# Differential attention: the difference of the two softmaxes on GpSimd, the eviction of the transposed probabilities on VectorE

## Chip, core and metric

The kernel runs on one core of one Trainium2 chip. The metric is the device time of one execution in microseconds, the median of several runs. Engines are called PE (TensorE), DVE (VectorE), ACT (ScalarE), POOL (GpSimd) and SP (SyncE, which issues the transfers).

## What is computed

A two-layer backbone over 256 context and 256 latent tokens of width 1024: layer 0 has scan and retention heads and a dense feed-forward, layer 1 has differential attention and two of eight experts per token. Everything is in 32-bit floats. The change lies in the attention of layer 1 alone, which has 8 heads; each head has two maps of keys and queries (64 wide each), 256 latent queries and 512 keys:

```python
def diff_attend(q, k, v, lam):
    s = jnp.einsum('bqhmd,bkhmd->bhmqk', q, k).astype(jnp.float32)
    p = jax.nn.softmax(s, axis=-1)
    a = p[:, :, 0] - lam.astype(jnp.float32) * p[:, :, 1]
    return jnp.einsum('bhqk,bkhe->bqhe', a.astype(v.dtype), v)
```

The output of a head is then normalised by its root mean square and goes through the output projection; after that a router picks experts and the weights of all eight experts are read.

## The kernel before

Layer 1 projects keys, queries and values, runs attention over heads 0 to 3 (the first half) and normalises and transposes those heads' outputs (`attended(0)`), does a little for the router, runs heads 4 to 7 and `attended(1)`, and then multiplies with the output projection (L194 to L196 with `oh`, three matmuls for each product of split operands). Weights come as 128x1024 tiles that ACT and DVE split into a high and a low part (L183, L184).

Attention itself is a loop over heads and, inside, over the two tiles of 128 queries: sixteen steps, called steps 0 to 15 here. A step, for each of its two maps m, forms 128x512 scores on PE (L1138) in one of four PSUM banks (`mm`, two for each query tile), takes the negated row maximum on DVE (L1139) and the exponential with its row sum on ACT (L1141) into tile `s0` or `s3`. The softmaxes are not divided out: the difference is kept in units of the first map's sum, so one factor per row, -lambda times the first sum over the second, is formed on DVE (L1143 the reciprocal, L1144 the product), and L1145 computes p0 = p1 * factor + p0 in one DVE instruction. L1147 puts the norm's epsilon into the same units. Four PE transposes (L1151) turn p0 by 128-column blocks into one PSUM bank (`tr`, two banks), L1153 evicts that bank to `s1` or `s2` on ACT, four accumulating matmuls multiply by the values (L1156), and ACT takes the sum of squares and the copy of the result (L1158, L1160).

Tiles `s0`, `s3` and the statistics `ast` have two buffers each, so two steps are in flight. The order of the instructions on each engine is not written out: a scheduler plans it when the kernel is built, from the dependences, the free buffers and the order of the program, and each engine then runs its list in that order. Transfers are issued from SP's list in the same way. The experts' first weights are loaded ahead into the big tiles as these come free; among them are those of the keys (`kT1`) and of the queries and outputs.

Of the kernel before, what the change touches and what calls it, by code (L numbers as in the profile page):

```python
# [14 lines left out]
AF = mybir.ActivationFunctionType  # L15
ALU = mybir.AluOpType
# [949 lines left out]
class Layer1(Layer0):  # L966
# [159 lines left out]
    def attention(self, heads):  # L1126

        nc = self.nc
        v = nc.vector
        for h in heads:  # L1130
            for t in range(2):
                qs = slice(P * t, P * t + P)
                st = self.scr("ast", (P, 6))
                p = []
                for m in range(2):
                    r = slice(64 * m, 64 * m + 64)
                    ps = self.mm(2 * t + m)
                    nc.tensor.matmul(ps, self.qT1[r, h, qs], self.kT1[r, h, :], start=True, stop=True)  # L1138
                    v.tensor_reduce(st[:, m:m + 1], ps, axis=AX.X, op=ALU.max, negate=True)  # L1139
                    e = self.scr(f"s{3 * m}")  # L1140
                    nc.scalar.activation(e, ps, AF.Exp, bias=st[:, m:m + 1], accum_out=st[:, 2 + m:3 + m])  # L1141
                    p.append(e)
                v.reciprocal(st[:, 4:5], st[:, 3:4])  # L1143
                v.scalar_tensor_tensor(st[:, 5:6], st[:, 2:3], self.lam, st[:, 4:5], op0=ALU.mult, op1=ALU.mult)  # L1144
                v.scalar_tensor_tensor(p[0], p[1], st[:, 5:6], p[0], op0=ALU.mult, op1=ALU.add)  # L1145

                v.scalar_tensor_tensor(self.o_eps[:, h // 4, t, h % 4:h % 4 + 1], st[:, 2:3], EPS, st[:, 2:3],  # L1147
                                       op0=ALU.mult, op1=ALU.mult)
                pt = self.tr()
                for c in range(4):  # L1150
                    nc.tensor.transpose(pt[:, P * c:P * c + P], p[0][:, P * c:P * c + P], self.ident)  # L1151
                at = self.scr(f"s{1 + t}")
                nc.scalar.activation(at, pt, AF.Copy)  # L1153
                po = self.acc()
                for c in range(4):
                    nc.tensor.matmul(po[:, 0:P], at[:, P * c:P * c + P], self.v1[:, c, P * h:P * h + P],  # L1156
                                     start=c == 0, stop=c == 3)
                nc.scalar.activation(self.scr("s5", (P, D), BF16)[:, 0:P], po[:, 0:P], AF.Square,  # L1158
                                     accum_out=self.o_ss[:, h // 4, t, h % 4:h % 4 + 1])
                nc.scalar.activation(self.o[:, t, P * h:P * h + P], po[:, 0:P], AF.Copy)  # L1160
# [398 lines left out]
```

## Time and profile before

| | us |
|---|---|
| median of 3 runs (1999.22 to 1999.8) | 1999.28 |
| the profiled execution | 1992.13 |
| its span, first to last instruction | 1990.0 |
| mean granted clock of TensorE, share of full | 0.988 |
| attention in the profiled span | about 1012 to 1083 |

The span is cut into 40 slices on the page, and each digit there is the busy share of an engine in tenths. Groups of instructions are named by line, engine and operation, with the tile written and the tiles read. The timeline gives the start and the duration of an instruction (or of several alike in a row, with their count) and in brackets the idle time of its engine before it and what ended that. Granted clock 1.00 is 2.4 GHz, 0.50 is 1.2 GHz.

### The profile page before, as it was taken

The page shows a single profiled execution, that of the slowest core. Times are in us where ns is not written, and L with a number is a line of the kernel's source. Part 1 is how long each engine was busy: PE and PEld are TensorE (multiplying, and loading weights), DVE is VectorE, ACT ScalarE, POOL GpSimd, SP SyncE. Part 2 cuts the span into 40 slices and gives each one's busy share as a digit, 9 for nine tenths or more (in the row PEclk, how much of TensorE's full clock was granted, in tenths as well). Part 3 has the DMA queues.
Part 4 walks back from the last instruction along what each step waited for, and adds up shares of the span by engine and source line. Part 5 has one row for each costly group of instructions (what it writes and reads, how often), then busy time and mean ns, then how long its engine had stood idle before and what let it go on. Part 6 is the DMA issues. An engine that isn't in the chain of part 4 may idle for free.

```text
span 1990.0 us, 26467 instructions
## 1 busy us (share of the span) xinstructions
PE 1909.2 (96%) x9936; PEld 1385.0 (70%) x9936; DVE 1120.0 (56%) x2011; ACT 815.4 (41%) x1286; POOL 10.1 (1%) x12
## 2 busy tenths in 40 slices
PE   6999999999999999999999999999999999999986
PEld 4776777778788888877766755876488656876341
DVE  5568668845876565667856306971298307970000
ACT  5535355542423322235455215861287316860100
POOL 0000000000000000000000000000000000000100
PEclk9999999999999999999998799999999999999999
DMA  8332434442655455532433499999999999999997
GB/s 322 118 96 96 148 117 142 145 143 75 203 166 172 154 173 189 178 101 85 132 133 113 160 418 418 416 355 394 417 417 393 364 417 417 417 340 411 417 417 316
DMA packets 103863, 502.67 MB, mean 253 GB/s; under 512 B 13104, under 2 KB 13744, under 8 KB 69296
## 3 DMA queue, kind: packets, MB, share of 16 engines
q1 hardware_dynamic: 103728, 500.91, 66.8%
q8 instruction: 80, 1.31, 0.3%
q14 instruction: 55, 0.45, 0.1%
HBM read 495.62 MB, written 5.24 MB: 252 GB/s over the span
## 4 chain that ended last, share of the span: by engine, by line
PE 74%; DMA 16%; DVE 6%; ACT 3%; issue 1%; SPq 0%; ACTq 0%; DVEq 0%
PE mm L195 16%; PE mm L196 16%; PE mm L194 16%; PE mm L1451 7%; DMA wide<-exp_d 5%; DMA wide<-exp_gu 5%; DMA raw<-exp_d 3%; PE acc L195 2%; PE acc L196 2%; PE acc L194 2%; DVE lo L184 1%; PE acc L315 1%; PE tr L1362 1%; PE acc L1465 1%; PE tr L1478 1%
## 5 line engine op out<-in xcount | busy, mean ns | idle before, releaser
L183 ACT ACTIVATE hi<-raw 128x1024 fp32r<-128x1024 f32 x208 | 220.2, 1060 | 402.6 <-PE mm L196 197.8
L184 DVE TENSOR_TENSOR lo<-raw,hi 128x1024 fp32r<-128x1024 f32 x208 | 253.7, 1223 | 175.3 <-ACT hi L183 169.9
L184 DVE TENSOR_TENSOR lo<-wide,hi 128x1024 fp32r<-128x1024 f32 x202 | 244.9, 1224 | 22.2 <-ACT hi L183 5.9
L183 ACT ACTIVATE hi<-wide 128x1024 fp32r<-128x1024 f32 x202 | 212.7, 1061 | 52.8 <-PE mm L196 34.0
L1451 PE MATMUL mm<-wide,q 128*64 128x256 f32 x1760 | 212.6, 386 | 8.5 <-DMA wide<-exp_gu 8.4
L1451 PEld LDWEIGHTS mm<-wide,q 128*64 128x64 f32 x1760 | 125.0, 138 | 82.8 <-DMA wide<-exp_gu 14.3
L194 PE MATMUL mm<-hi,hh 128*128 128x512 f32 x416 | 168.2, 405 | 1.7 <-DVE b L856 1.3
L195 PE MATMUL mm<-lo,hh 128*128 128x512 f32 x416 | 164.4, 395 | 0.1
L196 PE MATMUL mm<-hi,hl 128*128 128x512 f32 x416 | 163.3, 395 | 0.0
L1456 DVE TENSOR_TENSOR s<-s,mm 128x256 f32<-128x256 f32 x35 | 14.8, 422 | 252.1 <-ACT s L1454 252.1
L194 PE MATMUL mm<-h2h,hi 128*128 128x512 f32 (+1 forms) x376 | 142.2, 378 | 1.3 <-ACT hi L183 1.3
L195 PE MATMUL mm<-h2l,hi 128*128 128x512 f32 (+1 forms) x376 | 141.5, 377 | 0.0
L196 PE MATMUL mm<-h2h,lo 128*128 128x512 f32 (+1 forms) x376 | 141.1, 376 | 0.0
L195 PE MATMUL mm<-lo,q 128*128 128x512 f32 x336 | 133.0, 396 | 1.3 <-DVE lo L184 1.3
L196 PE MATMUL mm<-hi,q 128*128 128x512 f32 x336 | 131.3, 391 | 0.0
L1465 PE MATMUL acc<-wide,ef 128*64 128x512 f32 x456 | 111.7, 600 | 17.0 <-DMA wide<-exp_d 16.9
L194 PE MATMUL mm<-hi,q 128*128 128x512 f32 x336 | 112.9, 392 | 0.0
L194 PEld LDWEIGHTS mm<-hi,hh 128*128 128x128 f32 x416 | 78.2, 188 | 27.6 <-issue 9.7
L1465 PEld LDWEIGHTS acc<-wide,ef 128*64 128x64 f32 x456 | 32.8, 136 | 87.8 <-issue 52.2
L195 PEld LDWEIGHTS mm<-lo,hh 128*128 128x128 f32 x416 | 78.3, 188 | 17.0 <-issue 2.0
L196 PEld LDWEIGHTS mm<-hi,hl 128*128 128x128 f32 x416 | 78.0, 188 | 16.8 <-issue 0.8
L341 DVE SCALAR_TENSOR_TENSOR s<-raw,cond,s 128x512 f32<-128x512 f32 x112 | 80.4, 749 | 1.2
(393 smaller groups left out, 3243.7 us busy)
## 6 DMA issues: line engine op xcount, KB each, us to landing
wide<-exp_gu SPq DMA_DIRECT2D x177, 1024.0 KB, 14.4
wide<-exp_d SPq DMA_DIRECT2D x91, 1024.0 KB, 15.0
raw<-exp_gu SPq DMA_DIRECT2D x92, 512.0 KB, 14.7
raw<-odd_wmod SPq DMA_DIRECT2D x48, 512.0 KB, 4.2
raw<-w_in SPq DMA_DIRECT2D x44, 512.0 KB, 3.7
raw<-ffn_gu SPq DMA_DIRECT2D x44, 512.0 KB, 4.4
raw<-exp_d SPq DMA_DIRECT2D x42, 512.0 KB, 15.1
raw<-even_wmod SPq DMA_DIRECT2D x36, 512.0 KB, 3.8
```

The source lines that it names most:

```text
L183: nc.scalar.activation(hi, raw, AF.Copy)
L184: nc.vector.tensor_tensor(lo, raw, hi.bitcast(F32), op=ALU.subtract)
L194: mm(ps, lh, rh, start=first, stop=False, skip_group_check=skip)
L195: mm(ps, lh, rl, start=False, stop=False, skip_group_check=skip)
L196: mm(ps, ll, rh, start=False, stop=last, skip_group_check=skip)
L315: nc.tensor.matmul(ps[r:r + 32, :], self.cond[:, k, :], raw[:, 512 * kk:512 * kk + 512], start=k < 4, stop=k >= 4)
L341: nc.vector.scalar_tensor_tensor(t, w, self.cond[:, k, i:i + 1], t, op0=ALU.mult, op1=ALU.add)
L1362: nc.tensor.matmul(pt[:, w * kk:w * kk + w], self.x[:, 2 + t, P * (k + kk):P * (k + kk) + P], pn[:, t, 0:w], start=t == 0, stop=t == 1)
L1451: behind = mm(ps[s, 256 * g:256 * g + 256], xg[:, k, :], raw[i][:, c:c + 256], start=k + g == 0, stop=k == KD - 1, skip_group_check=True)
L1456: v.tensor_tensor(t, sg, ps[:, 256:512], op=ALU.mult)
L1465: mm(py[s], ap[:, f, :], raw[f - u][:, 512 * j:512 * j + 512], start=f == 0, stop=f == nd - 1, skip_group_check=True)
L1478: mm(pt, pT[s, P * t:P * t + P], y[s], start=True, stop=True)
```

## The change

The fused DVE instruction L1145 is replaced by two POOL instructions, a multiply of p1 by the factor (in place) and an add into p0; the eviction L1153 goes from ACT to DVE. Tiles, buffers and everything else in the program stay as they are; the planned order is made anew with the changed engines.

```diff
                 v.reciprocal(st[:, 4:5], st[:, 3:4])
                 v.scalar_tensor_tensor(st[:, 5:6], st[:, 2:3], self.lam, st[:, 4:5], op0=ALU.mult, op1=ALU.mult)
-                v.scalar_tensor_tensor(p[0], p[1], st[:, 5:6], p[0], op0=ALU.mult, op1=ALU.add)
+                nc.gpsimd.tensor_scalar(p[1], p[1], st[:, 5:6], None, op0=ALU.mult)
+                nc.gpsimd.tensor_tensor(p[0], p[0], p[1], op=ALU.add)
...
                 at = self.scr(f"s{1 + t}")
-                nc.scalar.activation(at, pt, AF.Copy)
+                v.tensor_copy(at, pt)
```

## Rows read from the trace of the kernel before

**Rows 1.** The page's slices: busy tenths of PE, busy share of the DMA engines.

```profile
PE   6999999999999999999999999999999999999986
...
DMA  8332434442655455532433499999999999999997
```

**Rows 2.** Windows: stretch, length, busy us (instructions) of PE, PEld, DVE, ACT, POOL, clock, DMA.

```profile
1012.00:1083.00 71.00, 64.27 (x301) 39.70 (x299) 43.78 (x117) 42.72 (x135) 0.00 (x0) 0.86 0.25 97
...
1144.00:1990.00 846.00, 802.96 (x4641) 522.27 (x4640) 376.10 (x392) 344.72 (x454) 9.93 (x8) 1.00 0.98 397
```

**Rows 3.** Timeline of SP's queue, the stretch from attention to the first expert.

```profile
1015.89 67.64 SPq L1401 DMA_DIRECT2D wide<-exp_gu  x6
...
1135.39 3.45 SPq L176 DMA_DIRECT2D raw<-exp_gu  x4
```

**Rows 4.** Chain that ended last, 1012 to 1084 us: shares by line.

```profile
by line: PE mm L1138 23.5%; PE acc L1156 19.9%; ACT s L1141 10.6%; PE tr L1151 10.1%; DVE ast L1139 8.9%; DVE s L1145 3.0%; issue 2.5%; PE acc L1174 2.3%; ACT s L1158 2.2%; ACT s L1153 2.1%; DVE lo L184 1.7%; PE tr L1083 1.5%; ACT hi L183 1
```

**Rows 5.** Groups, 1012 to 1083 us: xcount | busy us, mean ns | idle before, releasers.

```profile
L1145 DVE SCALAR_TENSOR_TENSOR s<-s,ast,s 128x512 f32<-128x512 f32 x16 | 12.0, 747 | 0.2
...
L1153 ACT ACTIVATE s<-tr 128x512 f32<-128x512 f32 x16 | 9.6, 601 | 3.5 <-PE tr L1151 3.5
```

**Rows 6.** Groups of POOL over the whole span.

```profile
L1415 POOL TENSOR_TENSOR rest<-x,rest 128x512 f32<-128x512 f32 x4 | 5.1, 1277 | 1883.0 <-ACT rest L358 1883.0
```

**Rows 7.** Groups of DVE: one input, two inputs, a copy out of PSUM.

```profile
L339 DVE TENSOR_SCALAR s<-raw,cond 128x512 f32<-128x512 f32 x16 | 7.6, 480 | 0.0
...
L1077 DVE TENSOR_TENSOR b<-b,ors 128x512 f32<-128x512 f32 x2 | 1.3, 687 | 0.0
...
L790 DVE COPY b<-tr 128x512 f32<-128x512 f32 x4 | 2.8, 688 | 4.0 <-PE tr L784 4.0
```

**Rows 8.** Timeline of POOL: the second instruction reads what the first wrote.

```profile
1890.82 1.27 POOL L1415 TENSOR_TENSOR rest<-x,rest 128x512 f32<-128x512 f32 x1
1892.18 1.27 POOL L1416 TENSOR_TENSOR rest<-rest,x 128x512 f32<-128x512 f32 x1
```

**Rows 9.** Timeline: difference and first transposes of steps 0 and 15.

```profile
1017.72 0.75 DVE L1145 SCALAR_TENSOR_TENSOR s<-s,ast,s 128x512 f32<-128x512 f32 x1
...
1018.68 1.05 PE L1151 MATMUL tr<-con,s 128*128 128x128 f32 x4
...
1078.24 0.75 DVE L1145 SCALAR_TENSOR_TENSOR s<-s,ast,s 128x512 f32<-128x512 f32 x1
...
1079.71 0.60 PE L1151 MATMUL tr<-con,s 128*128 128x128 f32 x4
```

**Rows 10.** Timeline of PE: products of two steps, first and last of the projection.

```profile
1067.91 1.06 PE L1156 MATMUL acc<-v,s 128*128 128x128 f32 x8
...
1070.45 1.06 PE L1156 MATMUL acc<-v,s 128*128 128x128 f32 x8
...
1076.75 0.47 PE L194 MATMUL mm<-hi,oh 128*128 128x512 f32 x1
...
1102.89 0.40 PE L196 MATMUL mm<-hi,oh 128*128 128x512 f32 x1
```

**Rows 11.** Windows of 2 us, columns as in rows 2.

```profile
1016.00:1018.00 2.00, 1.37 (x4) 0.59 (x4) 1.97 (x8) 1.87 (x5) 0.00 (x0) 1.00 1.02 420
1018.00:1020.00 2.00, 2.00 (x8) 0.99 (x6) 1.97 (x6) 0.48 (x3) 0.00 (x0) 0.70 0.81 303
...
1024.00:1026.00 2.00, 2.00 (x5) 0.68 (x3) 0.08 (x1) 1.68 (x7) 0.00 (x0) 0.59 0.51 213
...
1050.00:1052.00 2.00, 0.94 (x2) 0.29 (x2) 1.97 (x8) 0.78 (x2) 0.00 (x0) 1.00 0.00 0
1052.00:1054.00 2.00, 0.79 (x2) 0.50 (x2) 1.93 (x6) 0.78 (x2) 0.00 (x0) 0.73 0.00 0
...
1066.00:1068.00 2.00, 2.00 (x8) 0.95 (x7) 0.21 (x2) 1.74 (x7) 0.00 (x0) 0.85 0.00 0
```

**Rows 12.** Who waited for whom, 1012 to 1083 us: us, times, longest.

```profile
PE tr L1151 <- DVE s L1145: 0.2, 1, 0.2
```

## The prediction

> **What bounds the kernel now.** Read the slices of the page first [rows 1]: PE is busy nearly throughout, and from slice 23 (1144 us) to the end the DMA engines are full. Then two stretches of the windows [rows 2]: from 1144 us on the DMA share is 0.98, so the last 846 us take what the expert weights take; attention (1012 to 1083 us) has a DMA share of 0.25. Next the issuing queue [rows 3]: SP stands 67.64 us in a group of weight loads that begins at 1015.89 us, since the room they go to holds the keys of attention, and it resumes after its next long stop at 1135.39 us, when the first expert has begun to empty buffers. So the full-DMA stretch starts a fixed time after attention has ended: a microsecond lost or won on the way through attention is one at the end, and no transfer hides it.
>
> Inside attention no engine is full: in 71 us PE shows 64.27 busy, DVE 43.78, ACT 42.72 [rows 2]. The chain of waits over it [rows 4] alternates between PE (the scores L1138 23.5%, the products L1156 19.9%, the transposes L1151 10.1%), ACT and DVE. Of the two steps that change, it holds L1145 with 3.0% and L1153 with 2.1%; the window is 72 us, so 2.2 and 1.5 us. That is little beside their 12.0 and 9.6 us of busy time [rows 5]: most of each already lies beside PE.
>
> **The change part by part.** Sixteen times (8 heads by 2 query tiles):
>
> 1. *Removed from DVE:* L1145, 747 ns [rows 5], 12.0 us in all.
> 2. *Added to POOL:* a multiply of 128x512 by a column and an add of two such tiles. The add is priced by POOL's own row, 1277 ns for that shape and type [rows 6]. The multiply has no row on POOL. It is bounded below by DVE's one-input row, 480 ns [rows 7], and above by POOL's two-input 1277 ns. The nearest row is POOL's; but the multiply reads one tensor fewer, and on DVE that step goes from 687 to 480 ns, a factor of 0.70, so I take 1.27 x 0.70 = 0.89 us. Between a POOL instruction and the one that needs its result lie 0.09 us (1890.82 + 1.27 to 1892.18) [rows 8]. Together 0.89 + 0.09 + 1.27 = 2.25 us in place of 0.75: the difference p comes **1.5 us later** (1.1 with the low price, 1.9 with the high one).
> 3. *Moved from ACT to DVE:* the eviction, 601 ns on ACT [rows 5], 688 on DVE by its copy of the same shape out of the same kind of bank [rows 7]. So DVE's load stays (747 out, 688 in) and ACT's falls by 9.6 us.
>
> The Trainium skill speaks against part 2: "GPSIMD Engine Reference", section 4.1, sends elementwise work to the Vector engine, with GpSimd about two times slower for two inputs and roughly at line rate for one. The trace agrees on two inputs, 1.27 against 0.69 us. By that rate for one input (512 elements at the 1.2 GHz of the page's section 1, and some start) the multiply would be an estimated 0.6 us, and the sum below some 1.8 us lower; no run here shows that row yet.
>
> *Who waits.* Behind p on PE stand the four transposes of the same step; behind them in PE's order the scores of the step after next and the products. How much room a step has is read from the timeline: end of L1145 to the first L1151 of the same step. The first and the last of the sixteen pairs are shown [rows 9]. In order the gaps are 0.2, 2.9, 3.7, 1.7, 0.15, 0.16, 0.9, 0.7, then for the second half 13.3, 8, 4.1, 2.4, 0.7, 1.8, 0.7, 0.7 us. The wide ones lie where TensorE runs at half clock or where attention's halves meet. 0.15 is the bare hand-over, so the room is the gap less 0.15, and 1.5 us more come short by 1.45, 1.5, 1.5, 0.7, 0.9 (steps 0, 4, 5, 6, 7) and 0.95, 0.9, 0.9 (12, 14, 15): 8.8 us if all pass on. From that:
> - Steps 14 and 15 (1.8 us): beside them PE already takes up matmuls of the output projection, which at first need only the first four heads; its first L194 stands at 1076.75 and its last L196 at 1102.89 [rows 10]. What is pulled forward into the wait isn't missing later. Cost nothing; 1.8 us if the cover fails.
> - Step 0: the scores of step 2 (PE, 1.05 us at full clock, 2.0 at half) need only the exponentials, so they can go ahead of the late transposes: 1.0 of 1.45 covered.
>
> 8.8 - 1.8 - 1.0 = 6.0 us lost. *Gained:* an eviction on ACT waits there behind exponentials, and exponentials behind it; its 1.5 us on the chain [rows 4] go. L1145's 2.2 us on the chain are there because reductions of later steps queue behind it on DVE. The eviction takes that place, and it waits for PE, so I count nothing for them (2.2 us of gain if it finds a gap). **Sum: +4.5 us**; with the low price of the multiply the same sum gives +2.0, with the high one +7.4.
>
> *Queues and buffers.* POOL has no other work from its start to 1883 us [rows 6], so its wait for the factor (L1144) holds up nothing. On DVE the eviction waits for the transposes, and the reductions (L1139) and the factors of later steps stand behind it; ACT's exponentials wait for those. The statistics tile and the second exponential's tile (two buffers each) come free by POOL's instructions instead of L1145, some 0.1 and 1.5 us later; their next writers come two steps on. Steps follow each other at 2.54 us where they are fastest (products at 1067.91 and 1070.45 [rows 10]), so that is 5 us on; and POOL's 2.16 us of work fit into a step, barely. No DMA is moved past anything.
>
> **Rivals.**
> *Half clock.* TensorE falls from 2.4 to 1.2 GHz twice in attention [rows 11]: behind a slice in which PE was busy 1.37 of 2 us, and again behind one with 0.94. By the granted clocks of the slices (0.70 down to 0.50 and back over 0.59; 0.73 down and back over 0.85) it then ran some 6.8 and 13.7 us at half. Longer waits for p between 1030 and 1047 us could bring a third such stretch, which costs half its length, 3.4 to 6.9 us, on top of 4.5: about +9.6. For it: steps 4 to 7 lose most there. Against: PE's gaps there are short today. "TensorE: Matmul & The Clock Gate", section "HAM oscillation", in the Trainium skill tells of loops in which a wait returns each round and each round starts throttled; that both falls here came behind waits agrees with it.
>
> *Hidden by another order.* The order on each engine is planned when the kernel is built; with p later, PE may be given the scores of the step after next ahead of the transposes everywhere, as I assumed for step 0. They take 1.05 us, so the tight steps (0, 4, 5, 6, 7, 12) would lose 0.45, 0.45, 0.45, 0, 0 and 0, 1.35 in all, less the 1.5 of ACT: about 0 (-1 to +2). For it: L1145 made PE wait only 0.2 us in total [rows 12]. Against: today PE takes the transposes first.
>
> *Faster.* The order falls as above and the eviction finds DVE free, so L1145's 2.2 us go as well. One of its three places on the chain is where attention's halves meet: there DVE is the limit (1050 to 1054 us: 1.97 and 1.93 busy of 2 [rows 11]) and PE waits, and with L1145 off that queue the waits ahead of the second half-clock stretch get shorter. If that halves the stretch's cost of 6.9 us, the time is 0 - 2.2 - 3.4 = -5.6 us. It decides at PE's two waits of 1050 to 1054 us: from where they are gone. Against: they hang on reductions and on the first half's norm too, which stay on DVE, and the eviction's input comes 1.5 us later than today.
>
> *The change does not do what it says:* the eviction is not cheaper on DVE (688 against 601 ns), so what is saved is ACT's time alone, and ACT, at 42.72 of 71 us, is not the limit. That is inside the first sum.
>
> **How the numbers follow.** The profiled execution took 1992.13 us (span 1990.0 and 2.1 around it); the median of the runs is 1999.28, 7.2 more. The sum is made on the former, 1992.1 + 4.5 = 1996.6, and carried over to the median as a difference: 2003.8. Some 0.2%, 4 us, is what a measurement here can tell from no change.
> Chances: the forecast (+2.0 to +7.4) 0.50, of which 0.32 above 4 us; half clock 0.18, all above; another order 0.18, all within; faster 0.14 (-2.2 to -9), of which 0.11 below -4 us. So slower 0.32 + 0.18 = 0.50, same 0.18 + 0.18 + 0.03 = 0.39, faster 0.11. The range goes from -4.3 to +9.7, 1995.0 to 2009.0: the whole forecast, the other order and the nearer part of the half-clock and the faster case, so that some 0.18 stay outside. The forecast alone is 2001.3 to 2006.7.
>
> **What would show it.** In the changed profile: POOL's multiply near 0.9 us and its add near 1.27; p to transposes at the bare hand-over in steps 4 to 7, with PE waiting for POOL (in the table of waits, a row of transposes from POOL of some 4 to 7 us); the last score matmul, and with it SP's long stop, some 4 us later; the same shift at the first expert and at the end. If the transposes wait for POOL less than 2 us, the order has hidden it. If a slice at 0.50 stands between 1030 and 1047 us, the clock rival is in. If DVE waits for the transposes (its eviction behind PE) as long as ACT did, the gain is gone. The forecast is wrong altogether if the shift at the end is not that of the last score matmul.

## The result, and the profile after

The changed kernel takes 2025.16 us (median of 4 runs, 2017.24 to 2027.02) against 1999.25 of the kernel before on the same chip: a ratio of 1.0143, 95% interval 1.0117 to 1.017. Timed again later, it gave 2015.93 against 1995.5, 1.010 (1.0063 to 1.0137). So it is 25.9 and 20.4 us slower by the medians, 20 to 29 by the ratios; the prediction was 4.5 us slower, and 2009.0 at most.

The profiled execution took 2017.24 us, with a span of 2015.5 and a mean granted clock of 0.981 (before 1992.13, 1990.0 and 0.988). Line numbers behind the change are one higher: L1145 is now the multiply and L1146 the add on POOL, L1148 the epsilon, L1152 the transposes, L1154 the eviction, L1157 the products. The page's slices, to be held against [rows 1]:

```profile
PE   7999999999999999999988999999999999999986
POOL 0000000000000000000053000000000000000100
PEclk9999999999999999999978799999999998999999
DMA  8333434442655555424322499999999999989997
```

Counted from 0, attention lies in slices 20 and 21, where POOL now shows 5 and 3 tenths. The DMA row is full from slice 23 on, as before; but a slice is longer now, so that this is at 1159 us and not at 1144. The windows (columns as in [rows 2]) give attention of the changed kernel and the rest behind it:

```profile
1011.00:1102.00 91.00, 72.72 (x297) 43.19 (x296) 46.56 (x116) 35.75 (x118) 45.08 (x32) 0.81 0.20 76
...
1163.00:2015.50 852.50, 809.88 (x4640) 524.70 (x4636) 376.06 (x392) 344.23 (x454) 9.91 (x8) 0.99 0.98 393
```

The last window is laid so that it holds as many matmuls as the last one of [rows 2], 4640 and 4641; it takes 852.5 against 846 us, and most of that difference comes back below. What grew most is attention: 20 us longer, with 45.08 us of POOL in it, and the clock down from 0.86 to 0.81. The instructions of one line, from first to last start, tell its ends: scores and products of the changed kernel, then the first matmul of the experts, and below that SP's long stop.

```profile
L1138 PE MATMUL mm<-kT,b x64: 589/693/1220, 1011.1 to 1092.5; 64*128 64x512 f32 x64
...
L1157 PE MATMUL acc<-v,s x128: 273/275/582, 1025.7 to 1101.3; 128*128 128x128 f32 x128
...
L1452 PE MATMUL mm<-wide,q x1760: 378/379/690, 1139.8 to 1967.8; 128*64 128x256 f32 x196
...
1014.52 87.88 SPq L1402 DMA_DIRECT2D wide<-exp_gu  x6
```

Before, the same three were 1012.5 to 1074.9, the last product at 1081.9, and the first expert matmul at 1121.4. So attention, from its first score to its last product, grew from 69.4 to 90.2 us, **20.8 us**; SP's stop ends at 1102.40 in place of 1083.53 [rows 3], 18.9 later (attention begins 1.4 us earlier); the first expert matmul comes 18.4 later. From there the shift stays at 18.6 to 18.7 us until some 1670 us. Most of the rest, 6 us, arises in one spot between two experts:

```profile
1672.00:1674.00 2.00, 1.40 (x2) 0.50 (x2) 1.68 (x2) 1.59 (x2) 0.00 (x0) 0.65 1.00 414
1674.00:1676.00 2.00, 2.00 (x4) 1.16 (x4) 1.29 (x2) 0.00 (x0) 0.00 (x0) 0.50 1.04 430
```

TensorE falls to half clock there until 1687 us, in this execution and not in the one of before. Nothing ties it to the change: from first to last expert matmul the kernels of this study take 821.8 to 832.7 us in one profiled execution each, in no relation to what was edited that these profiles show (822.0 before, 828.0 after, 826.1 in a second profile of the changed kernel).

**What became of the parts.** Groups of the changed kernel in attention: POOL's pair, then on DVE the reductions, the eviction and the factor.

```profile
L1145 POOL TENSOR_SCALAR s<-s,ast 128x512 f32<-128x512 f32 x16 | 25.0, 1562 | 1052.2 <-DVE o_eps L1148 1033.2 <-DVE ast L1144 6.9 <-PE mm L1138 5.7
L1146 POOL TENSOR_TENSOR s<-s,s 128x512 f32<-128x512 f32 x16 | 20.2, 1262 | 1.2
...
L1139 DVE TENSOR_REDUCE ast<-mm 128x1 f32<-128x512 f32 x32 | 21.8, 688 | 18.7 <-PE mm L1138 12.3 <-POOL s L1145 6.1
L1154 DVE COPY s<-tr 128x512 f32<-128x512 f32 x16 | 11.0, 690 | 17.0 <-PE tr L1152 17.0
L1144 DVE SCALAR_TENSOR_TENSOR ast<-ast,lam 128x1 f32<-128x1 f32 x16 | 4.3, 266 | 1.8 <-ACT s L1141 1.5
```

The add (1262 ns) and the eviction (690) are as priced; the multiply is not: 1562 ns, above the upper bound of 1277 [rows 6]. And DVE stands idle 17.0 us ahead of its evictions, where ACT stood 3.5 [rows 5]. The table of waits of the same stretch:

```profile
DVE s L1154 <- PE tr L1152: 17.0, 15, 3.8
...
PE tr L1152 <- POOL s L1146: 11.3, 9, 2.5
ACT s L1141 <- PE tr L1152: 9.8, 5, 2.4
POOL s L1145 <- DVE ast L1144: 6.9, 4, 3.1
DVE ast L1139 <- POOL s L1145: 6.1, 7, 1.7
```

The chain over attention, which in [rows 4] went from PE to ACT and DVE, now goes through POOL, and the eviction, which the sum had taken off it, stands on it with 3.0% of 94 us, 2.8 us against 1.5 before:

```profile
by line: PE mm L1138 15.7%; POOL s L1145 13.7%; POOL s L1146 12.1%; PE tr L1152 11.6%; PE acc L1157 10.2%; issue 8.2%; DVE ast L1139 6.3%; DVE s L1154 3.0%; DVE ast L1144 2.5%; PE acc L1175 1.8%; PE mm L194 1.7%; PE mm L196 1.7%; ACT s L114
```

One turn of the timeline shows how these hang together:

```profile
1048.90 1.26 POOL L1146 TENSOR_TENSOR s<-s,s 128x512 f32<-128x512 f32 x1
...
1050.22 0.65 PE L1152 MATMUL tr<-con,s 128*128 128x128 f32 x4 [2.10 <-POOL s L1146]
...
1050.91 0.69 DVE L1154 COPY s<-tr 128x512 f32<-128x512 f32 x1 [1.36 <-PE tr L1152]
1051.52 0.21 DVE L1144 SCALAR_TENSOR_TENSOR ast<-ast,lam 128x1 f32<-128x1 f32 x1
...
1051.90 1.56 POOL L1145 TENSOR_SCALAR s<-s,ast 128x512 f32<-128x512 f32 x1 [1.74 <-DVE ast L1144]
```

PE waits for POOL's add (of step 6), DVE's eviction waits for PE, the factor of the next step stands behind that eviction in DVE's list, and POOL idles 1.74 us for the factor. It is a circle over three engines, in which each waits for the one before it, and it closes from one step to the very next. The chain over attention goes from an eviction by way of the factor to POOL's multiply five times (three times in the second profile of the changed kernel, below). In DVE's list the eviction of the step before stands ahead of the factor in 8 of 15 steps (in 5 where the eviction alone was moved). In other turns the circle closes without the eviction. Here the chain goes from the add of step 5 to the multiply of step 6: the scores of step 7 stand behind the transposes on PE, and the reduction that waits for them stands ahead of step 6's factor on DVE.

```profile
1042.94 1.27 POOL s L1146
...
1044.26 0.65 PE tr L1152 x4
1044.91 1.11 PE mm L1138 x4
...
1046.07 0.69 DVE ast L1139
...
1046.87 0.23 DVE ast L1144
...
1047.26 1.57 POOL s L1145
```

**Half clock.** It has a part of its own. The first stretch, which before lasted some 6.8 us [rows 11], goes from 1021 to 1037 us, into the time for which the rival of the prediction wanted a slice at 0.50, followed by shorter ones at 1051 to 1055 and 1065 to 1079. A slice of it:

```profile
1030.00:1032.00 2.00, 2.00 (x5) 0.63 (x4) 0.52 (x1) 0.73 (x3) 1.92 (x2) 0.50 0.00 0
```

### The profile page after: what moved, and what is told of

The parts are those of the page before. It is cut to its first block, busy times and chain, and to the rows that moved or that the text cites. A ratio compares the mean times of both kernels' runs of the same rounds, so it can differ in the third digit from the quotient of the medians.

```text
span 2015.5 us, 26535 instructions
## 1 busy us (share of the span) xinstructions
PE 1925.6 (96%) x9936; PEld 1390.9 (69%) x9936; DVE 1122.1 (56%) x2011; ACT 807.8 (40%) x1270; POOL 55.2 (3%) x44
## 4 chain that ended last, share of the span: by engine, by line
PE 75%; DMA 15%; DVE 6%; ACT 2%; issue 1%; POOL 1%; SPq 0%; POOLq 0%; ACTq 0%; DVEq 0%
PE mm L195 16%; PE mm L196 16%; PE mm L194 16%; PE mm L1452 9%; DMA wide<-exp_d 6%; DMA wide<-exp_gu 4%; DMA raw<-exp_d 2%; PE acc L195 2%; PE acc L196 2%; PE acc L194 2%; DVE lo L184 1%; PE acc L315 1%; PE tr L1479 1%; PE tr L1363 1%; PE acc L1466 1%
```

## The experiments

Every row below is one profiled execution's attention (first score to last product), the time in it that TensorE ran at half clock (from the granted clock of its 2-us slices), the length less half of that, called the path here, and the ratio of the timed runs. The path is an estimate: it takes all that lies in a half-clock stretch as twice as long, waits too. A "+" says what is added to the kernel named before it.

| kernel | attention | half clock | path | ratio, 95% interval |
|---|---|---|---|---|
| before | 69.4 | 20.5 | 59.2 | 1 |
| after | 90.2 | 34.2 | 73.1 | 1.0143 (1.0117 to 1.017) |
| after, a second time | 93.6 | 44.4 | 71.4 | 1.010 (1.0063 to 1.0137) |
| before + eviction on DVE | 65.1 | 10.2 | 60.0 | 0.9983 (0.9962 to 1.0004) |
| before + difference on POOL | 79.1 | 23.9 | 67.1 | 1.0053 (1.0031 to 1.0075) |
| before + difference on POOL, two-input multiply | 75.1 | 20.5 | 64.9 | 1.0029 (1.0006 to 1.0052) |
| after, two-input multiply | 81.3 | 23.9 | 69.4 | 1.007 (1.0044 to 1.0095) |
| after + a longer pair | 95.0 | 44.4 | 72.8 | 1.0152 (1.0118 to 1.0187) |
| before + POOL beside | 73.1 | 23.9 | 61.2 | 1.0024 (1.0 to 1.0047) |
| after + more statistics tiles | 90.5 | 37.6 | 71.7 | 1.011 (1.0081 to 1.0138) |
| after + deeper tiles | 78.7 | 23.9 | 66.8 | 1.0083 (1.0055 to 1.011) |
| after + order | 84.0 | 23.9 | 72.0 | 1.01 (1.0076 to 1.0125) |
| after + both | 74.7 | 23.9 | 62.7 | 1.0056 (1.0034 to 1.0077) |
| difference on POOL + DVE reader | 80.6 | 17.0 | 72.1 | 1.0086 (1.0052 to 1.012) |
| after + scores twice | 129.9 | 51.2 | 104 | 1.0282 (1.0248 to 1.0316) |
| before + eviction on DVE, order | 68.9 | 23.9 | 57.0 | 0.9981 (0.9962 to 1.0) |
| before + eviction on DVE, deeper tiles | 61.4 | 10.2 | 56.3 | 0.9955 (0.9937 to 0.9974) |

The kernel before alone varied from 1986.7 to 2004.4 us over 23 runs of one session, so single profiles of whole executions say little to 10 us. Attention's lengths follow the timed ratios to 1 us in some rows (75.1 less 69.4 is 5.7, and 0.29% of 1996 is 5.8) and only to 5 to 8 us in others: after, deeper tiles, order, both, and the DVE reader are all 5 to 8 us slower by their times than by their attention. In most of these the profiled execution was the quickest or nearly the quickest of the timed ones.

### One half of the change at a time

The eviction alone, in the kernel before:

```diff
-                nc.scalar.activation(at, pt, AF.Copy)
+                v.tensor_copy(at, pt)
```

> Only the eviction moves from ACT to DVE; the difference stays on DVE in one instruction. Theory latency (the POOL pair, 1.56 + 0.09 + 1.26 = 2.9 us where 0.75 us stood, lengthens the loop over two steps): attention, from the first score matmul to the last product, stays within 3 us of the 69.4 us of the kernel before, and the time within 4 us of it. Theory eviction (DVE, which waited 17.0 us for transposes in the changed kernel, holds the reductions up behind it): attention 5 to 10 us longer than before, and the time too.

Neither prospect came: attention is 65.1 us, 4.3 shorter; the time is 0.9983 of before (1993.42 against 1996.41), an interval that still holds no change. The path hardly moves (59.2 to 60.0), and half clock falls from 20.5 to 10.2 us, which is what the 4.3 are. DVE waits for the transposes 5.6 us here:

```profile
DVE s L1153 <- PE tr L1151: 5.6, 6, 2.4
```

The difference alone:

```diff
-                v.scalar_tensor_tensor(p[0], p[1], st[:, 5:6], p[0], op0=ALU.mult, op1=ALU.add)
+                nc.gpsimd.tensor_scalar(p[1], p[1], st[:, 5:6], None, op0=ALU.mult)
+                nc.gpsimd.tensor_tensor(p[0], p[0], p[1], op=ALU.add)
```

> Only the difference goes to POOL; the eviction stays on ACT. Theory latency: attention takes 85 to 92 us as in the changed kernel (90.2), and the time is 15 to 27 us above before. Theory eviction: less than half of the 20.8 us that attention grew by, so 70 to 80 us.

Attention 79.1, 9.7 longer, within the 70 to 80 of theory eviction; the time 1.0053, 10.6 us. PE's wait is nearly that of the whole change:

```profile
PE tr L1152 <- POOL s L1146: 9.6, 10, 2.5
```

The chain closes a circle here too, but over two steps: from the add of step 5 to the multiply of step 7, by way of the scores and the exponential of step 7.

```profile
1039.54 1.27 POOL s L1146
...
1040.86 0.66 PE tr L1152 x4
1041.51 1.11 PE mm L1138 x4
...
1042.67 0.70 DVE ast L1139
...
1043.46 0.56 ACT s L1141
...
1045.14 0.23 DVE ast L1144
...
1045.53 1.57 POOL s L1145
```

Two steps take 7.64 us there (1037.89 to 1045.53, from multiply to multiply), 3.82 a step. In the changed kernel the same steps 5 to 7 are 5.96 and 4.64 us apart, in both its profiles. Where ACT evicts, no eviction stands in DVE's list; a reduction of the next step stands ahead of the factor in 9 of 15 steps there and in 10 in the changed kernel. So the evictions are the greater part of what differs ahead of the factors.

Alone the halves give -4.3 and +9.7, together +20.8 (+24.2 in the second profile). So 15 us and more of attention (13 to 21 us by the timed ratios) appear only when both are made, and the eviction, a gain by itself, is the dearer half of the change once the difference is late. The runs below look for the reason.

### The price of the multiply

The same change with the multiply as a two-input instruction, the column of the factor spread over the row:

```diff
-                nc.gpsimd.tensor_scalar(p[1], p[1], st[:, 5:6], None, op0=ALU.mult)
+                nc.gpsimd.tensor_tensor(p[1], p[1], st[:, 5:6].to_broadcast([P, 512]), op=ALU.mult)
```

> The changed kernel with POOL's multiply written as a two-input one, the factor column read again for every element, in place of the multiply by a column, which took 1.56 us. Theory latency: if it takes POOL's two-input 1.27 us, the pair gets 0.3 us shorter, and 16 steps lose between half and all of that: attention 2 to 5 us shorter than 90.2. If the two-input form is no faster than 1.56 us, no change (within 2 us).

```profile
L1145 POOL TENSOR_TENSOR s<-s,ast 128x512 f32<-128x512 f32 x16 | 16.6, 1040 | 1052.0 <-DVE o_eps L1148 1031.7 <-DVE ast L1144 7.1 <-PE mm L1138 4.7
```

The same product takes 1.04 in place of 1.56 us. Those 0.52 us a step, 8.3 in all, take 8.9 us off attention (3.7 of it path, the rest half clock), more than the 2 to 5 expected, and bring the time to 1.007. With that multiply and the eviction left on ACT:

```diff
-                v.scalar_tensor_tensor(p[0], p[1], st[:, 5:6], p[0], op0=ALU.mult, op1=ALU.add)
+                nc.gpsimd.tensor_tensor(p[1], p[1], st[:, 5:6].to_broadcast([P, 512]), op=ALU.mult)
+                nc.gpsimd.tensor_tensor(p[0], p[0], p[1], op=ALU.add)
...
                 nc.scalar.activation(at, pt, AF.Copy)
```

> The difference on POOL with the faster two-input multiply (1.04 + 1.26 us), the eviction left on ACT. Theory latency: the difference alone gave 79.1 us of attention with 23.9 us of half clock; 0.52 us less on the path at half a pass for 16 steps is 4 us less: 73 to 76 us, still 4 us or more above the kernel before, and the time 4 to 7 us above before. If the eviction on ACT hides POOL by then: within 3 us of 69.4.

Attention 75.1, within the expected 73 to 76, time 1.0029. The difference of these two is the eviction: +6.2 us of attention with the quicker multiply, where it was +11.1 with the slow one and -4.3 with none on POOL. The timed ratios, which don't hang on one execution, say the same: 0.41% of 1996, 8.2 us, with the quicker one; 0.47 to 0.90%, 9 to 18 us, with the slow one; -0.17%, -3.4 us, with none.

In the other direction, a further POOL multiply (by a column of ones, 1039 ns) in the pair of the changed kernel:

```diff
                 nc.gpsimd.tensor_scalar(p[1], p[1], st[:, 5:6], None, op0=ALU.mult)
+                nc.gpsimd.tensor_tensor(p[1], p[1], self.con[:, C_ONE:C_ONE + 1].to_broadcast([P, 512]), op=ALU.mult)
                 nc.gpsimd.tensor_tensor(p[0], p[0], p[1], op=ALU.add)
```

> The changed kernel with one more POOL multiply in the pair, by a column of ones, two-input form, 1.04 us in the run before: the path through POOL goes from 2.9 to 4.0 us. Theory latency, with the slope between the two-input run and the changed one (0.52 us of path for 8.9 us of attention, of which 5.1 us are half clock): half of 1.13 us for 16 steps is 9, all of it 18; attention 99 to 108 us. If the planned order alone decided, and POOL's time did not: within 4 us of 90.2.

A miss: 95.0 us where 99 was the least expected, and 1.4 to 4.8 above the two profiles of the changed kernel, with the same path (72.8 against 73.1 and 71.4). So 0.52 us less gave a gain and 1.04 us more cost nearly nothing. What POOL adds is not simply multiplied by the steps; why it stops at this point was not found. The order of every list is planned anew for each kernel, which may be part of it.

### POOL's work beside, nobody waiting

The kernel before, with a multiply and an add of the same shapes on spare tiles whose result is not used:

```diff
+                side = self.scr("m0")
+                nc.gpsimd.tensor_scalar(side, self.one, self.o_eps[:, h // 4, t, h % 4:h % 4 + 1], None, op0=ALU.mult)
+                nc.gpsimd.tensor_tensor(side, self.one, side, op=ALU.add)
```

> The kernel before, with a POOL multiply and a POOL add of the same shapes per step that nobody waits for (they read a constant tile and write a spare one, and start from the finished epsilon column of the step; their result is not used). Theory sharing (POOL's work on SBUF holds DVE's instructions up, as L271 took 1.24 us instead of 0.17 beside POOL's add): DVE's L1145 and small instructions with operands in SBUF get longer, attention 4 us or more longer than 69.4. Theory latency: attention within 3 us of the kernel before, since nothing on the path waits for POOL.

Attention grows by 3.7 us, between the two prospects: 2.0 of path, the rest half clock. The time goes to 1.0024 (its interval touches no change). DVE's instructions in that profile:

```profile
L1147 DVE SCALAR_TENSOR_TENSOR s<-s,ast,s 128x512 f32<-128x512 f32 x16 | 13.1, 821 | 0.2
...
L1146 DVE SCALAR_TENSOR_TENSOR ast<-ast,lam 128x1 f32<-128x1 f32 x16 | 7.8, 488 | 2.8 <-ACT s L1143 2.5
```

The difference takes 821 in place of 747 ns [rows 5], and the factor, 216 ns before, 488. Nothing waits for POOL here, so these longer instructions are POOL's and DVE's sharing alone. The sum had no term for it; that it lengthens the whole is not clear of noise.

### Buffers and order

More statistics tiles, since the waits of the changed kernel show reductions behind POOL's multiply (6.1 us, above):

```diff
-                st = self.scr("ast", (P, 6))
+                st = self.scr("ast", (P, 6), bufs=6)
```

> The changed kernel with six statistics tiles in place of two, so that no reduction has to wait until POOL's multiply has read the factor out of an older one. Theory statistics tile (the 6.1 us in which DVE's reductions waited for POOL's multiply, and what follows from them): attention 5 us or more shorter than the 90.2 of the changed kernel, and no wait of L1139 for L1145 left. Theory latency: less than 3 us shorter, since the exponentials' tiles and PE's order still tie a step to the one before the last.

The wait has gone from the table, and the time has not: attention 90.5, 2016.18 us. DVE then waits 20.4 us at its evictions in place of 17.0. A wait that another takes over at once was no cause.

Four tiles for each map's exponentials, and the statistics as above:

```diff
-                    e = self.scr(f"s{3 * m}")
+                    e = self.scr((("s0", "s4", "s0", "s4"), ("s3", "m0", "s3", "m1"))[m][(2 * h + t) % 4])
```

> The changed kernel with four tiles in place of two for each map's exponentials, and six for the statistics, so that no step has to wait for tiles of the one before the last. Theory loop through the tiles: attention goes down by 8 us or more from 90.2, to 82 or less, since exponentials run ahead while POOL works. Theory order (what each engine's fixed list puts in front is what waits, above all the eviction ahead of reductions on DVE): less than 4 us.

Attention 78.7, 11.5 us shorter than after, as the loop through the tiles wanted it; path 66.8. The prediction had counted these tiles at nothing. In time the gain is smaller: 1.0083 against 1.010 and 1.0143, 3 to 12 us. The planned order changed with the tiles, too: the eviction of the step before stands ahead of the factor in 4 of 15 steps, where it was 8. So tiles and order aren't told apart by this run.

The second part of each step (transposes to the copy of the result) written behind the first part of the next, so that a factor stands ahead of the eviction of the step before it in the program:

```diff
+                if late is not None:
+                    self.behind(*late)
+                late = (h, t, p)
+        self.behind(*late)
```

> The changed kernel with the second part of a step (transposes, eviction, products, squares) written down behind the first part of the next step, so that in the planned lists scores, reductions and exponentials of the next step come ahead of it. Same instructions, tiles and engines. Theory order: attention 10 us or more shorter than 90.2, to about the 79.1 of the difference alone or below, with DVE's wait for transposes (17.0 us) down to under 8. Theory latency: less than 5 us shorter, the 2.9 us of the pair stay in the loop.

Attention 84.0, 6.2 shorter, between the prospects; the time, 1.01, is that of the changed kernel's second timing, so that a gain in time isn't shown. The planned list hardly follows: 6 of 15 factors still stand behind the eviction of the step before (8 in the changed kernel), and DVE's wait falls only from 17.0 to 13.1, so this is a weak test of the order:

```profile
DVE s L1163 <- PE tr L1161: 13.1, 12, 3.4
```

Both at once:

```diff
+                st = self.scr("ast", (P, 6), bufs=6)
...
+                    e = self.scr((("s0", "s4", "s0", "s4"), ("s3", "m0", "s3", "m1"))[m][(2 * h + t) % 4])
...
+                if late is not None:
+                    self.behind(*late)
+                late = (h, t, p)
```

> The changed kernel with both remedies at once: four exponential tiles per map and six statistics tiles (alone 11.5 us less of attention), and the second part of each step written behind the first part of the next (alone 6.2 us less). If they remove different parts of the loss, they add up: attention 70 to 75 us, time 1997 to 2004. If both only give the same loop more slack: 77 to 80 us, time 2004 to 2011.

Attention 74.7, in the range for "different parts", path 62.7; the time, 2005.7 or 1.0056, lies outside its range, in that of "the same loop". The eviction of the step before stands ahead of the factor in 3 of 15 steps. So with both, the whole change costs as much as the difference alone did without them (1.0053). The difference alone with the same slack was not run, so this does not show that the interplay of the halves is gone.

### Who is held by the eviction

The difference on POOL, the eviction on ACT, and a DVE copy of the same bank into a tile that nobody reads:

```diff
                 nc.scalar.activation(at, pt, AF.Copy)
+                v.tensor_copy(self.scr("m0"), pt)
```

> The difference on GpSimd and the eviction on ACT as in the kernel with the difference alone, and beside it a VectorE copy of the same transposed bank into a spare tile that nobody reads (0.69 us of VectorE each, work that the reference doesn't need). It separates two reasons for the 15 us of attention by which the two halves together cost more than one by one. Theory A, the place in VectorE's list: an instruction that waits there for the transposes, and with them for GpSimd, holds the reductions and the factor of later steps, and GpSimd and ACT wait for those. Then it makes no difference that ACT delivers the evicted tile: attention 84 to 93 us, VectorE waiting for transposes 12 to 18 us, time 2011 to 2022. Theory B, the evicted tile itself comes later to the products when VectorE writes it: attention as with the difference alone, 78 to 82 us, time 2003 to 2008.

```profile
DVE m L1155 <- ACT s L1154: 11.0, 11, 3.6
```

The evidence is split. Attention is 80.6 us, as theory B had it, with little half clock (17.0); its path is 72.1, that of the whole change (73.1 and 71.4) and 5.0 above the difference alone, as theory A has it; and the time, 1.0086, lies between the difference alone (1.0053) and the changed kernel (1.010 and 1.0143), inside A's range. The profiled execution was the quickest of five (2003.56; the others 2012.09 to 2019.3), so its attention is likely on the short side. That holds for the changed kernel's profile as well (2017.24; the others 2024.43 to 2027.02). The copy waited for ACT's eviction, not for the transposes themselves, and in the planned list it hardly stands where the eviction stood: the copy of the step before is ahead of the factor in 2 of 15 steps, not in 8, and the chain over attention never passes through it. At one of the two, step 6, the multiplies are 6.37 us apart where the difference alone has 3.82. So this run says little about theory A, and neither theory is shown by it.

### PE's own work, and the same kernel again

Each score matmul issued twice in the changed kernel, the second writing the same values over the first:

```diff
+                    nc.tensor.matmul(ps, self.qT1[r, h, qs], self.kT1[r, h, :], start=True, stop=True)
                     nc.tensor.matmul(ps, self.qT1[r, h, qs], self.kT1[r, h, :], start=True, stop=True)
```

> The changed kernel with each score matmul issued twice into the same bank, so that PE has 16 x 1.05 = 17 us more to do at full clock, 34 at half. Theory latency and clock (PE waits for POOL, and TensorE falls to half clock behind the waits): the added work lies in the waits, the half-clock stretches get shorter than the 34 us of the changed kernel, to 24 or less, and attention grows by less than 8 us, to 98 or less. Theory PE-bound: attention grows by 13 us or more.

The prospect of latency and clock is a miss, and the other, 13 us or more, is exceeded three times over: attention 129.9, 39.7 longer, where PE's busy time rose from 72.72 to 103.01, by 30.3; and half clock rose to 51.2.

```profile
1011.00:1142.00 131.00, 103.01 (x368) 56.72 (x366) 45.89 (x116) 36.92 (x117) 45.99 (x32) 0.80 0.14 53
```

The scores lie in the circle themselves, ahead of the reductions and so of the factors. The planned order changed as well: in this kernel the eviction of the step before stands ahead of the factor in all 15 steps, and in the last five of them POOL's multiplies are 6.83 to 6.84 us apart. So the run doesn't test PE's added work by itself.

The changed kernel, profiled again:

> The changed kernel itself, profiled a second time, to see how far one profiled execution speaks for the others. If attention's length belongs to the program: 88.5 to 92 us again, with half clock in the same three stretches, and the length of the expert stage may differ by several us. If the half clock in attention falls by chance: length 83 to 97 us with other stretches. Time 2017 to 2027.

Attention 93.6 with 44.4 us of half clock in four stretches, none of them between 1030 and 1047 us, a path of 71.4. So neither prospect held quite: the path repeats within 2 us, while the half clock moves by 10 us, worth 5, from one execution to the next. A difference of a few us between two attention lengths above can be no more than that. Its time, 2015.93, is slightly below the expected 2017.

### The eviction alone, with slack

The order of above, with the eviction on DVE and the difference left on DVE:

```diff
-                nc.scalar.activation(at, pt, AF.Copy)
+                v.tensor_copy(at, pt)
...
+                if late is not None:
+                    self.behind(*late)
+                late = (h, t, p)
```

> A candidate: only the eviction on DVE (that run gave 65.1 us of attention against 69.4), with the second part of a step written down behind the first part of the next. Theory order: attention 60 to 64 us, 0 to 5 less than the eviction alone, and the time 4 to 9 us below before. Theory latency has nothing to say here, as POOL is not used; if PE's work is the bound already (2.57 us a step at full clock, 41 us in all, and the half-clock stretches), no change from 65.1.

1991.24 us, 0.9981: as the eviction alone (0.9983), with attention at 68.9, where neither prospect had it (path 57.0, half clock 23.9). And the eviction alone with the deeper tiles of above, the program's order as it was:

```diff
+                st = self.scr("ast", (P, 6), bufs=6)
...
+                    e = self.scr((("s0", "s4", "s0", "s4"), ("s3", "m0", "s3", "m1"))[m][(2 * h + t) % 4])
...
-                nc.scalar.activation(at, pt, AF.Copy)
+                v.tensor_copy(at, pt)
```

> A candidate: the eviction on DVE, the difference on DVE as before, four tiles for each map's exponentials and six for the statistics. Theory loop through the tiles: exponentials run further ahead, PE waits less, attention 58 to 63 us against 65.1 of the eviction alone, the time 5 to 10 us below before. If PE and the meeting of the halves bound it: within 2 us of 65.1, the time about 3 us below before.

1987.61 us (12 runs, 1983.95 to 1993.55), **0.9955** (0.9937 to 0.9974), attention 61.4 as expected (58 to 63). This beats both kernels. Its gain is 9 us, of which the profile shows 8.0 in attention: 2.9 in the path and 5.1 in half clock. Against the eviction alone (0.9983) the tiles give 0.28%, with a planned list in which the eviction of the step before stands ahead of the factor in 2 of 15 steps in place of 5. How much of it they would give without the eviction was not tried.

## Why the prediction was wrong, point by point

**Right: where a microsecond of attention goes.** Attention +20.8, SP's stop +18.9, first expert +18.4: one to one within 2.4 us, of which 1.4 are an earlier start, as read from [rows 2, 3]. The sign that the prediction gave for this, the same shift at the last score matmul and at the end, holds less well: 17.6 and 25.5 us, with the 6 us of half clock between two experts in it. Right too: the add (1.26), the eviction on DVE (690 ns), the hand-over, and that PE would wait for POOL; it does so 11.3 us, where 4 to 7 were put down.

**Wrong: the price of the multiply.** 0.89 us was taken and 1.27 was the bound; it is 1.56. The step that failed is that of scaling by DVE's ratio of one to two inputs, and with it the bound itself: it took for granted that on POOL, too, one tensor fewer can't cost more. The trace contradicts here what the Trainium skill says in "GPSIMD Engine Reference", section 4.1, that one input goes at roughly line rate: 1.56 us with one tensor and a column, 1.26 with two tensors. The pair takes 1.56 + 0.09 + 1.26 = 2.91 us, p comes 2.16 us later and not 1.5. Nor does POOL's work fit into the fastest step of 2.54 us, as the prediction had it, "barely", with 2.16.

**Right in total only: the room of each step.** Put 2.16 into the same list of gaps: 15.4 us short, less 3.2 for steps 14 and 15 and 1.0 for step 0, gives +11.2; the difference alone measured +9.7. For the two-input multiply (1.04 + 0.09 + 1.26, so 1.64 later) the list gives 10.2 - 2.2 - 1.0 = +7.0, and +5.7 was measured. Both totals lie 1.3 to 1.5 high, but the steps do not agree. Timed from the first score to the first transposes of each step, the difference alone loses 3.6 us at step 2, where the list had more room than was needed; nothing at steps 4 and 5, where it had 2.16 and 2.15; and 1.7 at steps 14 and 15, which were to be covered. So the agreement of the totals is luck in part, and "all pass on" isn't shown. What the trace shows is the circle over two steps above: its way, transposes and then the scores of the step after next, is the one that the prediction named.

**Wrong by most: the eviction.** This is the step that failed by most: the sum counted the eviction as 1.5 us of gain and its place in DVE's list at nothing, as replaced like for like. By the runs its price has no sign of its own: -4.3 us with p on time, +6.2 with p 1.64 us late, +11.1 (+14.5 by the second profile) with p 2.16 late. From +11.2 - 1.5 = +9.7, which the right multiply would have given, to +20.8 and +24.2, the eviction's price is what is missing, with the half clock that came with it. The prediction did write down that the eviction waits for the transposes and that reductions and factors stand behind it; it gave this no price. The old L1145 didn't wait for PE. What took its place in DVE's list waits for POOL by way of PE, and in 8 of 15 steps the next factor for POOL stands behind it, so that the circle closes over one step (5.96 and 4.64 us) and not over two (3.82 a step). The sign named for it in the prediction, DVE waiting as long for the transposes as ACT did (3.5 us), came in nearly five times over, 17.0.

**Wrong: the tiles.** "Their next writers come two steps on" was reckoned from the fastest steps at the length they had. For the statistics it was harmless, as their own run shows; for both kinds of tiles together 11.5 us of attention came back, 3 to 12 us by the timed ratios, with an order that had changed as well.

**The half-clock rival came in on top.** It was given 3.4 to 6.9 us at 0.18; the two profiles show 34.2 and 44.4 us of half clock against 20.5, half of which is +6.9 and +12. It came on top of the sum, not in its place. That longer waits brought it is not shown: the order run and the DVE reader have paths as long (72.0 and 72.1) with 23.9 and 17.0 us of half clock, and the two profiles of one kernel differ by 10. The difference alone added 1.7 us of it, the eviction alone took 5.1 off. By the path the changed kernel is 12.2 to 13.9 us longer.

**Missing: sharing between POOL and DVE.** No term; 3.7 us of attention by the run with POOL beside (2.0 of path), with a time that is not clear of no change. What there is of it is contained in the +9.7 of the difference.

The other rivals did not come in: PE's transposes waited, so no other order hid the change, and nothing was faster. The range failed because its upper end added the half-clock price to a sum in which the eviction, the largest term as it turned out, was held to be a small gain with a spread of 2 us.

What stays open: that the two halves cost more together is shown by runs, and the traces show the circle by which they do. How much of it is the place of evictions and reductions in DVE's list, and how much the tiles held meanwhile, is not told apart, since most edits also changed the planned order; the run made to isolate the first hardly put its copy into that place; and the longer pair cost nearly nothing where the shorter one gained.

## What to carry to other kernels

Ask of every instruction that changes its engine what it will wait for there and what in that list stands behind it, above all whether something behind it feeds the very chain that it waits for: then two edits that are cheap apart close a circle, and the price of one depends on the other. Price an operation by a row of that engine with the same form (tensor by a column isn't tensor by tensor), and where there is none, let the bound reach past the neighbour. Where order is planned anew for each edit, count in the trace what stands ahead of what before a difference between two kernels is put down to the edit. And try more buffers: with deeper tiles the eviction alone became a gain of 0.45%.

## What the runs showed of the hardware

**POOL's multiply by a column** costs 1562 ns for 128x512 floats, the add of two tensors 1262, and the same multiply as a two-input instruction with the column spread over the row 1040 (1039 by a constant column).

**Some of DVE's instructions on SBUF run until POOL's has ended.** In the changed kernel:

```profile
1018.17 1.26 POOL L1146 TENSOR_TENSOR s<-s,s 128x512 f32<-128x512 f32 x1
1018.73 0.72 DVE L1144 SCALAR_TENSOR_TENSOR ast<-ast,lam 128x1 f32<-128x1 f32 x1
...
1061.69 1.27 POOL L1146 TENSOR_TENSOR s<-s,s 128x512 f32<-128x512 f32 x1
1061.74 1.24 DVE L271 TENSOR_SCALAR rs_m<-rs_m 128x8 f32<-128x8 f32 x1
```

The first DVE instruction takes 0.72 us against 0.22 elsewhere and ends at 1019.45, POOL's at 1019.43; the second takes 1.24 against 0.165 in the kernel before and ends with POOL's at 1062.98 and 1062.96. The reductions, which read PSUM, keep their 0.69 us beside POOL, and so does the reciprocal its 0.16. The Trainium skill, "GPSIMD Engine Reference", section 1, says that POOL's way into SBUF is shared with VectorE, with contention for instructions of two SBUF inputs or in a two-port mode; the trace agrees for the first instruction, which has two SBUF inputs. The second has one, and no run here shows in which mode it runs. The rows show how long one instruction is held.

**Half clock varies between executions of one program**: 34.2 and 44.4 us in attention, and from 821.8 to 832.7 us for the expert stage across kernels that don't differ there.
